# A one-core transformer layer: where two matrices' block sums are formed, and four small edits beside it

## The chip, the core and the metric

The kernel runs on one core of a Trainium2 chip. The metric is device time in microseconds (us) for one call, the median of several executions. Engines: PE multiplies matrices, DVE, ACT and POOL work on elements, SP issues nearly all DMAs.

## The reference

One layer (DEPTH = 1) on a 1024 x 1024 activation `x`, float32, 1024 frames in chunks of 64:

```python
h = rmsnorm(x, norm_mix_g)
qa, fa, ia, ga, qb, kb, vb, gate_a, gate_b = split(h @ w_in)          # w_in: 1024 x 5632
oa = hgrn2_mixer(qa, fa, ia, ga, ...)       # 4 heads of 128, decayed recurrence over chunks
ob = band_attention(qb, kb, vb, ...)        # 8 heads of 64, own chunk and 8 before it
merged = sigmoid(gate_a) * (oa @ w_branch_a) + sigmoid(gate_b) * (ob @ w_branch_b)
x = x + merged @ w_out
h2 = rmsnorm(x, norm_ffn_g)
x = x + (silu(h2 @ w_ffn_gate) * (h2 @ w_ffn_up)) @ w_ffn_down        # width 2816
h3 = rmsnorm(x, norm_ple_g)
x = x + sigmoid(h3 @ w_ple_gate) * (p @ w_ple_proj)
```

## The kernel before

Activations lie with features on the 128 partitions and 1024 frames along the free axis. Every float32 operand of a large product is split into a rounded part and a remainder (`wh`/`wl` for weights, whi/wlo for their halves and sums), and a product is three matmuls: hi x hi, hi x lo, lo x hi. ACT casts the rounded part, POOL or DVE subtracts to get the remainder.

The large products use a scheme with seven block products in place of eight (Strassen's, in a form with the sums S1 to S4 of weight blocks and T1 to T4 of activation blocks; `KINDS` lists the order A11, S2, A12, S3, S1, A22, S4).

The order of work on each engine is the program's order: `Pinned` and `order` chain each engine's instructions, and the generators (`yield`) say what is written between which products. The stages and about where they lie in the profile:

- `first_norm`, then `hgrn_in` and `hgrn_mix` for four heads, woven together: until about 310 us. `hgrn_in` projects, `hgrn_mix` runs the recurrence by levels (products of DVE, transposes through PE, copies of ACT). `hgrn_mix` copies the transposed keys with ACT at L447.
- `attention`: until about 527 us.
- `gate_units`: six units of seven products each for the mixer's gates, until about 690 us; then `branches`, `out_proj`, `first_part` and `second_part`.
- `ff_pairs`: 22 units n = 0 to 21, alternately gate and up, 84 matmuls each, about 893 to 1290 us (n = 0 is done in `second_part`). In a unit `strassen` writes seven `product`s into three PSUM banks b1 to b3; behind each, DVE adds a bank to a sum (`u2 = p1 + b2` behind product 1, two sums behind product 3, and so on), and `next(side)` lets one step of side work follow: `strassen_weights` prepares the next unit's weights, `keep_acts` stores the activations for the down product. Product 3 adds to the bank b2 that u2 was read from, so PE may start it only when DVE has made u2. DVE works in order, so what stands ahead of such a sum delays it.
- `ff_down` (seven passes with `passes`), then `ple`, seven passes again, with `side` doing norms and output work between the steps.

The sums S1 to S4 of the weights of `w_out` (four jobs, `oq`) and `w_ffn_down` (eleven jobs, `wq`) are formed ahead of their products: load four blocks, four additions, store the sums in DRAM (`spill`). `QUADS` = 8 jobs are done by `quad_early` beside the recurrence: `quad_piece` cuts a job in two halves, each one load, four additions of 128x256 on POOL (L1093), four stores; `beside` takes one step of it per step of `hgrn_in`. The other seven are done by `quad_slow` in `gate_units`, with four POOL additions of 128x512 a job (L1068 to L1079).

`unit_gate` makes a gate: DVE multiplies by the row of norms `rb`, ACT takes the Sigmoid, POOL multiplies twice. `Small` pools hold rings of temporaries: `FFN` (tmp, raw, q512, q1024), `MIXER`, `SMALL`. `weights(n, ahead)` loads the next weights into two raw buffers, which come free when POOL has made the remainder. In `ple`, `out` makes one block of the output in four steps (DVE product, ACT Sigmoid, DVE product, final add and DMA), `some(4)` takes one step of four such streams, and `m_split` casts and subtracts the next activation operand, which `operand` otherwise does when fewer than two are ready.

Of the kernel before, what the change touches and what calls it, by code (L numbers as in the profile page):

```python
# [17 lines left out]
P = 128  # L18
# [13 lines left out]
RAW = 2  # L32
AHEAD = 3
PLAIN = 4
QUADS = 8


C_MIX, C_FFN, C_PLE, C_ON, C_GQ, C_GK, C_LB = 0, 8, 16, 24, 25, 26, 27
# [18 lines left out]
class Trunk:  # L57
# [175 lines left out]
    def setup(self):  # L233
        nc, d = self.nc, self.d
        cp = self.cp
        self.cols = cp.tile([P, N_COL], F32, name="cols")
        nc.scalar.dma_start(self.cols, d["cols"])
        self.eye = cp.tile([P, P], F32, name="eye")
        self.ones = cp.tile([P, 1], F32, name="ones")
        nc.vector.memset(self.ones, 1.0)  # L240
        self.onesr = cp.tile([P, P], F32R, name="onesr")
        nc.vector.tensor_copy(self.onesr, self.ones[:, :].to_broadcast([P, P]))
        self.mhalf = cp.tile([P, 8], F32, name="mhalf")
        nc.vector.memset(self.mhalf, -0.5)
# [20 lines left out]
    def first_norm(self):  # L265

        nc = self.nc
        self.u = []
        outs = [self.mm() for _ in range(4)]
        start = [self.unit() for _ in range(2)]  # L270
        ws = [(hi, lo) for hi, lo, _, _ in start]
        for k in range(KC):
            x = self.slot()
            sc = self.cols[:, C_MIX + k:C_MIX + k + 1]
            if k == 0:

                hi, lo = self.slot(F32R), self.slot(F32R)
                h0, h1 = slice(0, HALF), slice(HALF, T)
                self.load(x[:, h0], self.d["x"][k][:, h0])
                for unit in start:  # L280
                    self.unit_piece(unit, 0, 2 * P)
                self.load(x[:, h1], self.d["x"][k][:, h1])
                for h in (h0, h1):
                    self.A.activation(hi[:, h], x[:, h], AF.Copy, scale=sc)
                    nc.vector.scalar_tensor_tensor(lo[:, h], x[:, h], sc, f32(hi[:, h]), ALU.mult, ALU.subtract)
                self.u.append((hi, lo))
            else:
                self.load(x, self.d["x"][k])
                self.u.append(self.split(x, sc, self.A))
            if k == 1:  # L290
                for unit in start:
                    self.unit_piece(unit, 2 * P, D)
            if k == 3:
                self.load(self.eye, self.d["eye"])
                self.load(self.masks, self.d["masks"])
# [12 lines left out]
        return outs  # L308
# [486 lines left out]
    def gate_units(self, sums):  # L795
# [42 lines left out]
        for n in range(units):  # L838

            def side():  # L840
                more = self.strassen_weights() if n + 1 < units else self.branch_first()
                if n == 0:
                    yield
                    yield
                next(more, None)
                if n + 2 < units:
                    self.strassen_load()
                yield
                for i, _ in enumerate(more):
                    for _ in range(1 + i % 2):  # L850
                        next(sums, None)
                    yield

            self.strassen(lambda c, half, ps: self.gate_done(PLAIN + 2 * n + c, half, ps), side(), early=n == 0)
# [225 lines left out]
            yield  # L1080
        store(*prev)

    def quad_piece(self, src, k, sums, half):

        G, cols = self.nc.gpsimd, HALF // 2
        w = self.slot(late=True)
        at = slice(half * cols, half * cols + cols)
        self.load(w[:, :].rearrange("p (i c) -> p i c", i=4), src.rearrange("p (i c) -> p i c", i=4)[:, :, at])
        for _ in range(5):
            yield  # L1090
        a11, a21, a22, a12 = [w[:, i * cols:i * cols + cols] for i in range(4)]
        for out, x, y, op in ((a22, a21, a22, ALU.add), (a21, a11, a21, ALU.subtract), (a11, a22, a11, ALU.subtract), (a12, a12, a11, ALU.subtract)):
            G.tensor_tensor(out, x, y, op)  # L1093
            yield
        yield
        to = slice(k % 2 * HALF + at.start, k % 2 * HALF + at.stop)
        for kind, part in zip(("S2", "S3", "S1", "S4"), (a11, a21, a22, a12)):
            if k % 2 == 0 and half == 0:
                sums[kind, k // 2] = self.spill()
            self.store(sums[kind, k // 2][:, to], part)  # L1100
        yield
        yield

    def quad_early(self, jobs):

        pieces = [self.quad_piece(*job, half) for job in jobs for half in range(2)]
        live = []
        while pieces or live:
            if pieces:
                live.append(pieces.pop(0))  # L1110
            for _ in range(6):
                for x in list(live):
                    if next(x, x) is x:
                        live.remove(x)
                yield

    def quad_plan(self, plain, npairs, sums):
# [286 lines left out]
    def unit_gate(self, c, half, ps):  # L1404
# [2 lines left out]
        hs = slice(half * HALF, half * HALF + HALF)  # L1407
        s = self.stmp()
        V.tensor_tensor(g[:, hs], ps, self.rb[:, hs], ALU.mult)
        A.activation(s, g[:, hs], AF.Sigmoid)  # L1410
        G.tensor_tensor(g[:, hs], g[:, hs], s, ALU.mult)
        G.tensor_tensor(g[:, hs], g[:, hs], self.rb[:, hs], ALU.mult)

    def unit_up(self, c, half, ps):
        hs = slice(half * HALF, half * HALF + HALF)
# [132 lines left out]
    def ff_pairs(self):  # L1548
        V, A, G = self.V, self.A, self.G

        units = len(self.sorder)
        self.acts = {}
        self.strassen_load()
        for n in range(1, units):
            if n % 2 == 0:
# [2 lines left out]
            def side():  # L1558
# [6 lines left out]
                yield  # L1565
                for _ in more:
                    next(keep, None)
                    yield
                drain(keep)

            self.strassen((self.unit_gate, self.unit_up)[n % 2], side())
            if n % 2 == 1:
# [28 lines left out]
    def down_first(self):  # L1601

        self.down_plan()
        self.ahead = 3
        self.weights(0, ahead=3)
        yield
        for _ in range(2):
            self.down_load()
            yield
        self.down_split()  # L1610
        self.down_load()
        yield
# [128 lines left out]
    def ple(self):  # L1741
# [32 lines left out]
        def after(kind, u, ps):  # L1774
# [10 lines left out]
            elif kind == "S1":  # L1785
                V.tensor_tensor(u3[u], ps, u3[u], ALU.add)
                V.tensor_tensor(ps, ps, u2[u], ALU.add)
                todo.append(out(2 * u + 1, h0, u3[u]))
            elif kind == "A22":
                todo.append(out(2 * u + 1, h1, ps))  # L1790
                next(todo[-1])
# [18 lines left out]
        def side():  # L1810
# [29 lines left out]
            yield  # L1840
            for i in range(4):
                some(4)
                yield
            del todo[:]

# [15 lines left out]
    def run(self):  # L1861
# [18 lines left out]
        with ExitStack() as es:  # L1880
# [10 lines left out]
            self.hg, self.ended, self.pend, self.qk, self.bias, self.ob = {}, [], [], {}, {}, []  # L1891
            self.oa = [None] * 4
            with ExitStack() as mixer:
                self.masks = mixer.enter_context(tc.tile_pool(name="levels", bufs=1)).tile([P, len(LEVELS), 64], U8, name="masks")
                outs = self.first_norm()
                self.xp = Small(tc, mixer, MIXER)
                self.late = mixer.enter_context(tc.tile_pool(name="late1", bufs=2))
                jobs = [(d["oq"][k], k, self.osums) for k in range(4)] + [(d["wq"][k], k, self.sums) for k in range(NFF // 2)]
                sums = self.quad_early(jobs[:QUADS])
                drain(beside(self.hgrn_in(0, outs), sums))  # L1900
                for h in range(3):
                    weave(beside(self.hgrn_in(h + 1), sums), self.hgrn_mix(h), 41500, 17000)
                self.feed = self.attn_in()
                weave(beside(chain(self.attn_v(), islice(self.feed, FIRST)), sums), self.hgrn_mix(3), 41500 + 1300 * FIRST, 17000)
                drain(sums)
                self.attn_setup()
                drain(self.attention())
            with ExitStack() as xs:
                self.qp = Small(tc, xs, QUARTERS, "gate_", reuse_waits="tile")
                self.fp = Small(tc, xs, FFN, "gates_", reuse_waits="tile")  # L1910
                drain(self.gate_units(self.quad_slow(jobs[QUADS:])))
            with ExitStack() as xs:
                self.late = xs.enter_context(tc.tile_pool(name="late", bufs=6, reuse_waits="tile"))
                drain(self.branches())
# [16 lines left out]
            drain(self.ple())  # L1931


SMALL = {"rb": 1, "rtok": 1, "epsv": 1, "state": 1, "t8": 2, "t4": 4, "mx2": 4, "den": 4}
QUARTERS = {"whiq": 3, "wloq": 3}
FFN = {"q1024": 1, "q512": 3, "raw": 2, "tmp": 8}
MIXER = {"s": 3, "pt": 4, "bias": 4, "qk": 4, "qs": 2, "sq": 1}


# [18 lines left out]
def beside(main, side):  # L1958
    for x in main:
        next(side, None)  # L1960
        yield x


def weave(main, side, main_ns, side_ns):
# [111 lines left out]
```

## Time and profile before

| | |
|---|---|
| median of three runs | 1590.09 us (1587.43, 1590.09, 1590.85) |
| profiled execution | 1588.19 us, span 1585.9 us |
| TensorE clock over the span | 0.996 |
| DMA | 230.40 MB, mean 145 GB/s |

In the rows, "A 12.0 (x3)" means busy for 12.0 us in 3 instructions; a group row gives count, busy us, mean ns of one, and the idle time before them with what ended it; in a timeline row stand start, duration, engine, line, operation and the tiles (out<-in). PEld is PE's weight load. Buffer numbers are left out of the names: `s` is a 128x1024 slot, `m` a small tile, `t` a temporary (stmp), `pm` a PSUM bank, `wr` raw weights, `q` sums of weights, `d` DRAM.

### The profile page before, as it was taken

How to read it: one execution, taken by the hardware profiler on the slowest of the kernel's cores; microseconds unless marked ns; L12 is line 12 of the kernel's file. 1: busy time of each engine (PE TensorE's matmuls, PEld its weight loads, DVE VectorE, ACT ScalarE, POOL GpSimd, SP SyncE). 2: the span in 40 equal slices, each digit the busy share in tenths (PEclk: the TensorE clock that was granted, in tenths of full speed). 3: DMA queues.
4: the chain of work that ended last, by engine and by line, in shares of the span. 5: the costliest groups of instructions: out<-in, count | busy, mean ns of one | idle time of the engine just before them, and what ended most of it. 6: DMA issues, size and time to landing. Idle time of an engine off the chain costs nothing.

```text
span 1585.9 us, 21744 instructions
## 1 busy us (share of the span) xinstructions
PE 1559.4 (98%) x8224; PEld 1311.1 (83%) x8224; DVE 1166.6 (74%) x1670; ACT 639.8 (40%) x1057; POOL 802.0 (51%) x461
## 2 busy tenths in 40 slices
PE   8999999999999999999999999999999999999997
PEld 6898888878888888888888888888888888888886
DVE  5656675468778778644898988888888856765658
ACT  6321211157777643421377322232222234445453
POOL 3764542123113059625330877777777754645454
PEclk9999999999999999999999999999999999999999
DMA  5443220220113358675244433333333278885344
GB/s 189 138 156 119 90 97 27 66 89 27 48 41 107 140 191 306 239 292 212 71 149 172 159 100 100 100 100 113 104 112 107 89 255 321 296 274 196 126 133 158
DMA packets 92649, 230.40 MB, mean 145 GB/s; under 512 B 9856, under 2 KB 26880, under 8 KB 92032
## 3 DMA queue, kind: packets, MB, share of 16 engines
q1 hardware_dynamic: 92400, 229.00, 42.1%
q8 instruction: 64, 1.05, 0.3%
q14 instruction: 41, 0.34, 0.1%
q10 hardware_dynamic: 144, 0.02, 0.0%
HBM read 163.70 MB, written 65.27 MB: 144 GB/s over the span
## 4 chain that ended last, share of the span: by engine, by line
PE 80%; DVE 6%; DMA 6%; POOL 4%; issue 2%; ACT 2%; SPq 1%; POOLq 0%; ACTq 0%; DVEq 0%
PE pm L83 77%; DVE s L54 3%; PE pm L86 3%; POOL wl L126 2%; DMA d<-s 1%; POOL s L1093 1%; DMA s<-in_oq 1%; DMA wr<-d 1%; DVE m L54 1%; SPq L78 1%; DMA wr<-in_qk 1%; DVE q L54 0%; POOL s L54 0%; ACT wh L123 0%; DMA wr<-in_fm 0%
## 5 line engine op out<-in xcount | busy, mean ns | idle before, releaser
L83 PE MATMUL pm<-s,wh 128*128 128x512 f32 (+1 forms) x1712 | 532.1, 392 | 6.6 <-ACT wh L123 5.2
L83 PE MATMUL pm<-s,whi 128*128 128x512 f32 x1568 | 483.0, 389 | 0.6 <-DVE t L54 0.6
L126 POOL TENSOR_TENSOR wl<-wr,wh 128x1024 fp32r<-128x1024 f32 (+2 forms) x108 | 269.5, 2500 | 321.1 <-ACT wh L123 314.9
L83 PEld LDWEIGHTS pm<-s,wh 128*128 128x128 f32 x1712 | 319.9, 189 | 73.5 <-ACT wh L123 5.6
L83 PEld LDWEIGHTS pm<-s,whi 128*128 128x128 f32 x1568 | 294.2, 188 | 61.9 <-DVE t L54 1.0
L83 PE MATMUL pm<-s,wl 128*128 128x512 f32 (+1 forms) x856 | 334.1, 390 | 0.3 <-POOL wl L126 0.3
L54 DVE TENSOR_TENSOR s<-s,s 128x512 f32<-128x512 f32 (+4 forms) x213 | 255.9, 1230 | 92.4 <-ACT s L54 58.3
L83 PE MATMUL pm<-s,wlo 128*128 128x512 f32 x784 | 305.2, 389 | 0.0
L83 PE MATMUL pm<-wh,s 128*128 128x256 f32 (+1 forms) x896 | 239.3, 341 | 0.0
L123 ACT CAST wh<-wr 128x1024 fp32r<-128x1024 f32 (+2 forms) x114 | 114.7, 1007 | 261.7 <-PE pm L83 132.8
L83 PEld LDWEIGHTS pm<-s,wl 128*128 128x128 f32 x856 | 161.3, 188 | 34.8 <-POOL wl L126 1.4
L83 PEld LDWEIGHTS pm<-s,wlo 128*128 128x128 f32 x784 | 147.2, 188 | 31.1 <-DVE wlo L54 0.5
L83 PEld LDWEIGHTS pm<-wh,s 128*128 128x128 f32 x896 | 155.4, 191 | 13.8
L83 PE MATMUL pm<-wl,s 128*128 128x256 f32 (+1 forms) x448 | 148.0, 330 | 0.4 <-POOL wl L126 0.4
L54 DVE TENSOR_TENSOR t<-pm,t 128x512 f32<-128x512 f32 x138 | 94.7, 686 | 71.4 <-PE pm L83 69.3
L54 POOL TENSOR_TENSOR wlo<-wr,whi 128x512 fp32r<-128x512 f32 (+1 forms) x53 | 109.9, 2083 | 72.2 <-ACT whi L54 72.2
L54 DVE TENSOR_TENSOR s<-pm,s 128x512 f32<-128x512 f32 (+1 forms) x134 | 87.3, 680 | 79.9 <-PE pm L83 78.7
L54 ACT CAST whi<-q 128x512 fp32r<-128x512 f32 (+1 forms) x81 | 61.5, 759 | 160.3 <-DVE q L54 140.5
L54 POOL TENSOR_TENSOR s<-s,t 128x512 f32<-128x512 f32 x44 | 76.6, 1741 | 81.7 <-ACT t L54 81.7
L54 ACT CAST s<-s 128x1024 fp32r<-128x1024 f32 (+1 forms) x94 | 90.2, 980 | 68.0 <-DVE s L54 33.7
L54 POOL TENSOR_TENSOR wlo<-q,whi 128x512 fp32r<-128x512 f32 x52 | 89.0, 1712 | 19.0 <-ACT whi L54 19.0
L83 PEld LDWEIGHTS pm<-wl,s 128*128 128x128 f32 x448 | 85.9, 192 | 5.9 <-POOL wl L126 0.6
(146 smaller groups left out, 1953.5 us busy)
## 6 DMA issues: line engine op xcount, KB each, us to landing
s<-d SPq DMA_DIRECT2D x67, 512.0 KB, 6.0
d<-s SPq DMA_DIRECT2D x115, 256.0 KB, 3.3
wr<-d SPq DMA_DIRECT2D x36, 512.0 KB, 3.7
s<-in_wq SPq DMA_DIRECT2D x22, 512.0 KB, 5.6
wr<-in_sg SPq DMA_DIRECT2D x22, 512.0 KB, 4.1
wr<-in_su SPq DMA_DIRECT2D x22, 512.0 KB, 4.1
s<-in_x SPq DMA_DIRECT2D x21, 512.0 KB, 7.8
d<-s SPq DMA_DIRECT2D x18, 512.0 KB, 4.9
```

The lines of the kernel that those rows point to most:

```text
L54: return lambda *a, **k: self.trunk.order(op(*a, **k), self.key)
L78: return self.order(self.nc.sync.dma_start(out, ap), "sp")
L83: return self.order(self.nc.tensor.matmul(*a, **k))
L86: return self.order(self.nc.tensor.transpose(*a, **k))
L123: self.nc.scalar.copy(hi[:, c], raw[:, c])
L126: rest.tensor_tensor(lo[:, c], raw[:, c], f32(hi[:, c]), ALU.subtract)
L1093: G.tensor_tensor(out, x, y, op)
```

## The change

Seven edits. (1) `quad_early`, `quad_piece` and `beside` go; five jobs are done by `quad_slow` in `gate_units` (one step per product, where it was one or two in turn), and the other ten by the new `quad_pieces` in `ff_pairs`, in halves, with the additions on DVE and one buffer `quad`; `tmp` has 7 buffers instead of 8. (2) `unit_gate` uses Silu, and POOL multiplies once. (3) `down_first` loads two weights ahead, then activations, then the third weight. (4) In `ple`, `m_split` is called in four steps of `side`. (5) The final add of the S1 outputs is on DVE. (6) `onesr` stands before `ones`, `masks` has 8 x 64 bytes instead of 5 x 64. (7) `state` stands before `rtok` in `SMALL`.

```diff
-QUADS = 8
+QUADS = 5
...
+        self.onesr = cp.tile([P, P], F32R, name="onesr")
         self.ones = cp.tile([P, 1], F32, name="ones")
         nc.vector.memset(self.ones, 1.0)
-        self.onesr = cp.tile([P, P], F32R, name="onesr")
...
@@ gate_units
-                for i, _ in enumerate(more):
-                    for _ in range(1 + i % 2):
-                        next(sums, None)
+                for _ in more:
+                    next(sums, None)
                     yield
@@ in place of quad_piece and quad_early
+    def quad_pieces(self, jobs):
+
+        V, cols = self.V, HALF // 2
+        for src, k, sums in jobs:
+            for half in range(2):
+                self.n += 1
+                w = self.fp.tile([P, 4 * cols], F32, tag="quad", name=f"qd{self.n}")
+                at = slice(half * cols, half * cols + cols)
+                self.load(w[:, :].rearrange("p (i c) -> p i c", i=4), src.rearrange("p (i c) -> p i c", i=4)[:, :, at])
+                yield
+                yield
+                a11, a21, a22, a12 = [w[:, i * cols:i * cols + cols] for i in range(4)]
+                V.tensor_tensor(a22, a21, a22, ALU.add)
+                V.tensor_tensor(a21, a11, a21, ALU.subtract)
+                yield
+                V.tensor_tensor(a11, a22, a11, ALU.subtract)
+                V.tensor_tensor(a12, a12, a11, ALU.subtract)
+                yield
+                for kind, part in zip(("S2", "S3", "S1", "S4"), (a11, a21, a22, a12)):
+                    if k % 2 == 0 and half == 0:
+                        sums[kind, k // 2] = self.spill()
+                    self.store(sums[kind, k // 2][:, k % 2 * HALF + at.start:k % 2 * HALF + at.stop], part)
                 yield
@@ unit_gate
-        A.activation(s, g[:, hs], AF.Sigmoid)
-        G.tensor_tensor(g[:, hs], g[:, hs], s, ALU.mult)
-        G.tensor_tensor(g[:, hs], g[:, hs], self.rb[:, hs], ALU.mult)
+        A.activation(s, g[:, hs], AF.Silu)
+        G.tensor_tensor(g[:, hs], s, self.rb[:, hs], ALU.mult)
@@ ff_pairs
+        pieces = self.quad_pieces(self.later)
...
                 for _ in more:
                     next(keep, None)
+                    if n > 1:
+                        next(pieces, None)
                     yield
                 drain(keep)
+                if n % 4 == 0:
+                    next(pieces, None)
+                if n == units - 2:
+                    drain(pieces)
@@ down_first
-        self.weights(0, ahead=3)
+        self.weights(0, ahead=2)
         yield
         for _ in range(2):
             self.down_load()
             yield
+        self.weights(0, ahead=3)
@@ ple
-                todo.append(out(2 * u + 1, h0, u3[u]))
+                todo.append(out(2 * u + 1, h0, u3[u], V))
...
             yield
             for i in range(4):
                 some(4)
+                self.m_split()
                 yield
             del todo[:]
@@ run
-                jobs = [(d["oq"][k], k, self.osums) for k in range(4)] + [(d["wq"][k], k, self.sums) for k in range(NFF // 2)]
-                sums = self.quad_early(jobs[:QUADS])
-                drain(beside(self.hgrn_in(0, outs), sums))
+                drain(self.hgrn_in(0, outs))
...
-                drain(self.gate_units(self.quad_slow(jobs[QUADS:])))
+                jobs = [(d["oq"][k], k, self.osums) for k in range(4)] + [(d["wq"][k], k, self.sums) for k in range(NFF // 2)]
+                drain(self.gate_units(self.quad_slow(jobs[:QUADS])))
+                self.later = jobs[QUADS:]
...
-SMALL = {"rb": 1, "rtok": 1, "epsv": 1, "state": 1, "t8": 2, "t4": 4, "mx2": 4, "den": 4}
+SMALL = {"rb": 1, "state": 1, "rtok": 1, "epsv": 1, "t8": 2, "t4": 4, "mx2": 4, "den": 4}
-FFN = {"q1024": 1, "q512": 3, "raw": 2, "tmp": 8}
+FFN = {"q1024": 1, "q512": 3, "raw": 2, "tmp": 7, "quad": 1}
```

More of the change, by code (lines that the diff above doesn't have):

```diff
@@ L294, in first_norm @@
                 self.load(self.eye, self.d["eye"])
-                self.load(self.masks, self.d["masks"])
+                self.load(self.masks[:, :len(LEVELS), :], self.d["masks"])
             if k:
@@ L1081, in quad_slow @@
         store(*prev)
[L1083 to L1114, printed above, removed]
+    def quad_pieces(self, jobs):
[19 more added lines that the diff above has]
+                    self.store(sums[kind, k // 2][:, k % 2 * HALF + at.start:k % 2 * HALF + at.stop], part)
@@ L1893, in run @@
             with ExitStack() as mixer:
-                self.masks = mixer.enter_context(tc.tile_pool(name="levels", bufs=1)).tile([P, len(LEVELS), 64], U8, name="masks")
+                self.masks = mixer.enter_context(tc.tile_pool(name="levels", bufs=1)).tile([P, 8, 64], U8, name="masks")
                 outs = self.first_norm()
@@ L1897, in run @@
                 self.late = mixer.enter_context(tc.tile_pool(name="late1", bufs=2))
-                jobs = [(d["oq"][k], k, self.osums) for k in range(4)] + [(d["wq"][k], k, self.sums) for k in range(NFF // 2)]
-                sums = self.quad_early(jobs[:QUADS])
-                drain(beside(self.hgrn_in(0, outs), sums))
+                drain(self.hgrn_in(0, outs))
                 for h in range(3):
-                    weave(beside(self.hgrn_in(h + 1), sums), self.hgrn_mix(h), 41500, 17000)
+                    weave(self.hgrn_in(h + 1), self.hgrn_mix(h), 41500, 17000)
                 self.feed = self.attn_in()
-                weave(beside(chain(self.attn_v(), islice(self.feed, FIRST)), sums), self.hgrn_mix(3), 41500 + 1300 * FIRST, 17000)
-                drain(sums)
+                weave(chain(self.attn_v(), islice(self.feed, FIRST)), self.hgrn_mix(3), 41500 + 1300 * FIRST, 17000)
                 self.attn_setup()
@@ L1955, in drain @@
             return e.value
[L1958 to L1961, printed above, removed]
 def weave(main, side, main_ns, side_ns):
```

## The prediction

> **What bounds the kernel now.** I read the page first, then busy times by stage, PE's waits, and then single stretches of the timeline in which PE waits or nearly does.
>
> ```profile
> span 1585.9 us, 21744 instructions
> PE 1559.4 (98%) x8224; PEld 1311.1 (83%) x8224; DVE 1166.6 (74%) x1670; ACT 639.8 (40%) x1057; POOL 802.0 (51%) x461
> ```
>
> PE is busy in all but 26.5 us of the span, and the change neither adds nor removes a matmul. So the change can only move those 26.5 us, plus time in which PE runs at a lower clock, or make PE wait where it doesn't wait now. Where they lie shows by stage (busy us of each engine, then clock, DMA share, GB/s):
>
> ```profile
> 43.00:240.00 197.00, 191.33 (x1405) 174.89 (x1404) 132.70 (x228) 43.93 (x79) 109.09 (x93) 0.99 0.37 121
> 527.00:690.00 163.00, 163.00 (x738) 134.64 (x735) 119.18 (x136) 68.11 (x99) 89.56 (x53) 1.00 0.72 251
> 866.00:893.00 27.00, 26.17 (x117) 21.53 (x117) 26.37 (x25) 16.13 (x25) 18.81 (x10) 0.94 0.59 195
> 893.00:1274.00 381.00, 381.00 (x1682) 315.57 (x1681) 334.18 (x308) 109.43 (x161) 286.05 (x163) 1.00 0.31 101
> 1556.00:1586.00 30.00, 19.63 (x98) 16.54 (x97) 24.98 (x34) 8.19 (x14) 15.74 (x10) 0.90 0.28 107
> 173.00:180.00 7.00, 6.74 (x44) 6.74 (x45) 1.77 (x7) 1.33 (x4) 1.44 (x2) 0.76 0.01 2
> ```
>
> The recurrence of the first three heads (43 to 240) holds 5.7 us of idle PE; the gate units of the mixer (527 to 690) hold none; the gate/up units of the feed-forward part (893 to 1274) hold none, though DVE is busy 88% there; the last 30 us hold 10.4. The last row is the one place in the recurrence with a lower clock: 7 us at 0.76 lose 7 x 0.24 = 1.7 us. So a change that empties the recurrence's side work can win at most 5.7 + 1.7 = 7.4 us there, and whatever it moves into 893 to 1274 can win nothing there and only lose.
>
> **The recurrence: 64 additions of POOL and their 80 DMAs go.** QUADS 8 with quad_early means 8 x 2 pieces of four additions.
>
> ```profile
> L1093 POOL TENSOR_TENSOR s<-s 128x256 f32<-128x256 f32 x64 | 55.8, 873 | 52.4 <-DMA s<-in_wq 24.4 <-DMA s<-in_oq 21.4 <-DMA d<-s 2.9
> PE pm L83 <- ACT s L447: 3.2, 2, 1.8
> PE pm L83 <- DVE s L54: 1.3, 3, 0.5
> PE pm L86 <- DVE s L54: 0.8, 1, 0.8
> 156.04 1.98 POOL L1093 TENSOR_TENSOR s<-s 128x256 f32<-128x256 f32 x2
> 157.98 2.82 POOL L126 TENSOR_TENSOR wl<-wr,wh 128x1024 fp32r<-128x1024 f32 x1
> 161.01 4.25 POOL L1093 TENSOR_TENSOR s<-s 128x256 f32<-128x256 f32 x4 [0.21 <-DMA s<-in_wq]
> 162.65 2.01 DVE L54 TENSOR_TENSOR m<-s,s 128x512 f32<-128x512 f32 x2
> 164.58 2.92 DVE L54 TENSOR_TENSOR s<-s,s 128x512 f32<-128x512 f32 x2
> L54 DVE TENSOR_TENSOR s<-s 128x512 f32<-128x512 f32 x10 | 6.8, 684 | 0.0
> 173.26 0.81 PE L83 MATMUL pm<-s,s 128*128 128x128 f32 x4 [1.76 <-ACT s L447]
> ```
>
> The second to fourth rows are PE's waits of this stage: for ACT's copy of the transposed keys, and for DVE's products. Both follow on DVE: ACT casts what DVE made. A 128x512 product of two SBUF tiles costs DVE 0.68 alone (the row of ten), and the pairs at 162.65 and 164.58 took 2.01 and 2.92 where 1.37 would do, the first and half of the second beside POOL's additions at 161.01. Of these 2.2 us of delay I put 1.2 down to L1093, and 0.7 more to its additions at 156.04 and around 169: 1.9 us of DVE lag ahead of PE's waits of 0.8 and 1.76 us. Without it PE's two waits there shrink by about 1.9, and with a shorter wait I expect the slow clock behind it (1.7) to go in most cases: 1.2. The same in the other heads: of the remaining 3.1 us of idle (5.7 - 2.6) I take half, 1.7. Sum **-4.8 us**; the ends are -1.3 (only half of 2.6: the split of weights at 157.98, 2.82 us, and the small splits stay on POOL and block DVE as before) and -7.4 (all). SP is passed by 16 loads and 64 stores fewer ahead of the weights; PE waits for no DMA here, so nothing is counted.
>
> **The mixer's gate units** get 5 whole jobs instead of 7, so eight additions fewer (row L1068 is one of four a job), at one step per product instead of one or two. FFN's tmp ring is 7, not 8: at the next unit's first copy it reuses u2 instead of p1, which DVE reads last some 3 us after the unit's end, while the copy comes 2.7 us after it. PE is idle for 0.0 of 163 us here, so there is no gain; 0 taken, ends 0 and +1.5 (six units at a quarter of a microsecond).
>
> ```profile
> L1068 POOL TENSOR_TENSOR s<-s,s 128x512 f32<-128x512 f32 x7 | 10.1, 1445 | 3.4 <-DMA d<-t 2.0 <-DMA d<-s 1.4
> L54 POOL TENSOR_TENSOR s<-s,rb 128x512 f32<-128x512 f32 x41 | 68.2, 1663 | 3.2
> L54 ACT ACTIVATE t<-s 128x512 f32<-128x512 f32 x44 | 27.8, 632 | 116.4 <-DVE s L54 112.4 <-issue 2.6 <-ACT whi L54 0.2
> L54 ACT ACT_TABLE_LOAD x2 | 2.6, 1283 | 0.0
> 1582.00 0.42 DVE L54 TENSOR_TENSOR s<-s,s 128x256 f32<-128x256 f32 x1
> d<-s SPq DMA_DIRECT2D x64, 128.0 KB, 3.8
> s<-in_wq SPq DMA_DIRECT2D x22, 512.0 KB, 5.6
> 990.94 1.42 DVE L54 TENSOR_TENSOR t<-pm,t 128x512 f32<-128x512 f32 x2 [1.44 <-PE pm L83]
> 996.38 0.69 DVE L54 TENSOR_TENSOR t<-pm,t 128x512 f32<-128x512 f32 x1 [0.17 <-PE pm L83]
> 997.83 2.88 DVE L54 TENSOR_TENSOR q<-wr,q 128x512 f32<-128x512 f32 x1
> 1005.74 0.68 DVE L54 TENSOR_TENSOR t<-pm,t 128x512 f32<-128x512 f32 x1
> ```
>
> **The gate/up units** lose one POOL multiplication per gate, 44 in all (41 of them in the row, 1.66 each: 68 us), because Silu does the work of Sigmoid and one product. No Silu is in the trace; the same shape takes 0.63 with Sigmoid, and I take that. It may need its table in and Sigmoid's back, 2 x 1.28 us on ACT, which is busy 29% of 893 to 1274 and idle before these activations: 0 taken, with no gain since no wait of PE here ends on ACT, and at most +1.3 ahead of 893, where DVE is full.
>
> They gain 10 jobs x 2 pieces = 20 pieces: 80 DVE additions of 128x256 at 0.42 (the row of the last stage) = 34 us, 20 loads and 80 stores on SP. DVE has 381 - 334 = 47 us free there, and POOL's relief gives some of its blocked time back, so there is room on the average. What counts is one deadline. The adds at 990.94 and 996.38 start when PE ends products 3 and 5 of a unit: 2.72 us a product. Product 1 of the next unit ends five products after 990.94, at 1004.5; its sum u2 ran at 1005.74 to 1006.42, and product 3, which adds to the same bank, is due at 1007.2. Slack 0.8 us. From 996.38 to 1006.42 DVE does eight operations, 5.4 us alone, in 10.0: 4.6 us are blocking, as at 997.83, where 0.68 became 2.88. A piece's pair (0.84) in this window would use the slack up, if POOL blocked as now; with one POOL operation in two gone from the gate's end it should block about a fifth less, 0.9. That cancels out: 0 for the additions.
>
> [...]
>
> The wait added: one buffer (quad: 1), so a load stands on SP behind the landing of its predecessor's four stores, and strassen_load and keep_acts' stores stand behind it for 3.8 us; those have a unit (19 us) of lead. The stores' issue (1.4), landing (3.8) and the load (5.6, less in this emptier stage) make 8 to 10.8 us from a piece's last addition to the next one's first; DVE comes to it three steps later, 8.2 us, or 13.6 where a unit's end lies between. With five steps a unit and four a piece I count 7 of 20 pieces with no unit's end between. DVE's queue would stand there for 0 to 2.6 us, the PSUM sums behind it, and PE behind those beyond the slack. I take 0.2 each: **+1.4 us**; ends 0 and 7 x 1.8 = +12.6.
>
> **Ahead of 893** and at the start of the down stage:
>
> ```profile
> 892.67 0.50 PE L83 MATMUL pm<-s,whi 128*128 128x512 f32 x1 [0.58 <-DVE t L54]
> 1320.81 0.50 PE L83 MATMUL pm<-s,wl 128*128 128x512 f32 x1 [0.34 <-POOL wl L126]
> 1263.69 13.01 SPq L78 DMA_DIRECT2D wr<-in_dw  x3
> ```
>
> The wait at 892.67 is the same u2 add, late behind POOL's gate products; with one of two gone I take it as gone, **-0.6** (ends -0.7, +0.7 with the table load). In down_first SP stood 13 us in three weight loads, the third waiting for a raw buffer, with the activations' loads behind it; with two loads first those start some 12 us sooner and crowd less at 1320: **-0.2** of 0.34 (ends -0.4, +0.4).
>
> **The last stage.** m_split is called once more in each of the four steps behind `some(4)`. Counting side()'s steps, these lie in the fourth product (S3), not the fifth. Three casts and remainders (T4 twice, B22's first) move from the two passes behind it to there. The final adds of the S1 outputs move from POOL to DVE.
>
> ```profile
> 1556.51 1.21 DVE L54 TENSOR_TENSOR s<-s,s 128x1024 fp32r<-128x1024 f32 x1
> 1557.65 4.70 DVE L54 TENSOR_TENSOR s<-s,rb 128x512 f32<-128x512 f32 x4
> 1563.98 5.82 DVE L54 TENSOR_TENSOR s<-s,s 128x1024 fp32r<-128x1024 f32 x5 [1.64 <-ACT s L54]
> 1565.89 6.32 POOL L54 TENSOR_TENSOR s<-s,s 128x512 f32<-128x512 f32 x4 [5.90 <-DVE s L54]
> 1569.73 2.48 DVE L54 TENSOR_TENSOR pm<-pm,rb 128x512 f32<-128x512 f32 x4
> ```
>
> From 1563.98 DVE is never idle for long until the end, so its lag is the tail. The remainder at 1556.51 (1.21) leaves; the one at 1563.98 stays (B22's second). ACT comes to its cast some 0.8 sooner. Then four products of 0.6 and four new adds of 0.6 take 4.8 where the row has 4.7 for the products alone, blocked by POOL's adds of 1.6: **-0.5 us**, ends -1.2 and +1.5 (the adds unhidden, POOL's blocking still there).
>
> **Alignment** moves onesr, state, masks and what lies behind them by some bytes.
>
> ```profile
> L83 PEld LDWEIGHTS pm<-m,onesr 128*128 128x128 f32 x24 | 4.5, 188 | 1.0
> L83 PEld LDWEIGHTS pm<-s,wh 128*128 128x128 f32 x1712 | 319.9, 189 | 73.5 <-ACT wh L123 5.6 <-DVE s L196 1.7 <-DVE s L285 0.8
> ```
>
> onesr now lies behind a tile of 4 bytes and loads in 188 ns, as long as the large tiles: 0.
>
> **The sum**: -4.8 - 0.6 - 0.2 - 0.5 + 1.4 = -4.7. The profiled execution took 1588.2 (span 1585.9 and 2.3 around it), which gives 1583.5; it stands 1.9 under the median of the three runs, 1590.1 (1587.4 to 1590.9), and against that median I say **1585.4 us**.
>
> **Rivals.** *The deadline of u2 (slower).* The additions of the pieces stand in DVE's queue ahead of the PSUM sums in all 16 units that carry pieces (5 steps a unit, 81 steps, from the third on). If POOL blocks as before, a unit is late by 0.84 - 0.8 plus one block of the short additions, some 0.7: 16 x 0.7 = 11.2, and 1590.1 - 6.1 + 11.2 = 1595.2. It decides from 0.4 us a unit on (6.4 us, the whole gain). For it: DVE's 88% and 0.8 us of slack; against it: 68 us fewer on POOL. Chance 0.27. [...]
> *The recurrence stays.* POOL's weight splits, now sooner, block DVE in the additions' place; only 1.3 is won there: 1590.1 - 1.3 - 1.3 + 1.4 = 1588.9. Chance 0.18.
> *All of it comes*: 7.4 in the recurrence, 0.6, 0.4 and 1.2 after it, no loss in the units: 1580.5. Chance 0.08.
>
> **How the numbers follow.** The forecast has 0.47, its own range 1582 to 1588.5. What a measurement of this kernel tells from no change is about 0.2%, 3.2 us: faster is under 1586.9. Faster: 0.38 of the forecast, 0.08, and 0.03 of the second rival, 0.49; within: 0.09 + 0.12 + 0.03 of the first, 0.24; slower: 0.24 + 0.03, 0.27. The range takes in the third rival and most of the first: 1580 to 1597.
>
> **What would show it.** Right: no L1093 row, idle of PE in 43 to 240 under 3 us and a clock of 1.00 there; POOL with one product per gate; DVE over 90% in the units and PE still without a wait; the last DVE add half a microsecond nearer to PE's end. Wrong: PE waits for DVE t in the units, DVE waiting there for a load of wq, or the waits for ACT's L447 as long as before.

## The result, and the profile after

The changed kernel takes 1609.49 us (median of 6 runs, 1607.23 to 1615.12) where the kernel before takes 1589.93 (6 runs): 1.0127 times as long, 95% interval 1.0099 to 1.0155. The forecast was 1585.4 and the range ended at 1597. The profiled execution took 1614.1 us, 4.6 more than the median.

The page after, its head and the first line of engines:

```profile
span 1611.1 us, 21725 instructions
...
PE 1568.1 (97%) x8224; PEld 1314.9 (82%) x8224; DVE 1165.9 (72%) x1754; ACT 639.6 (40%) x1059; POOL 649.6 (40%) x341
```

POOL is 152 us less busy, DVE as busy as before, and PE idles 43.0 us instead of 26.5. Busy times by stretch (recurrence, feed-forward units, and 16 us out of these), columns as in the prediction:

```profile
43.00:240.00 197.00, 195.11 (x1454) 179.66 (x1454) 123.46 (x229) 44.10 (x80) 54.33 (x29) 1.00 0.12 38
...
893.00:1296.00 403.00, 385.86 (x1662) 314.86 (x1661) 340.48 (x384) 104.31 (x156) 211.16 (x119) 0.98 0.44 147
1046.00:1062.00 16.00, 12.99 (x45) 10.16 (x44) 12.23 (x13) 1.98 (x3) 7.65 (x4) 0.79 0.28 98
```

The recurrence is now nearly full (1.9 us of idle PE instead of 5.7, clock 1.00). The gate/up units, in which PE had no idle time, have 17 us of it and a lower clock, although DVE is busy only 84% of the time and POOL only 52%. PE's waits in the units, after:

```profile
PE pm L83 <- DVE t L54: 17.1, 12, 3.0
```

Both traces hold all 8,224 matmuls, so the start of each can be compared with the start of the same one before. The differences below are worked out that way, by where the matmul stood before; "on POOL" is the version of the experiments with the additions on POOL.

| from .. to (us, before) | after | on POOL |
|---|---|---|
| start .. 45 | +2.1 | -0.6 |
| 45 .. 526 (recurrence, attention) | -7.3 | -7.5 |
| 526 .. 859 (mixer's gate units to the out projection) | +0.1 | +0.1 |
| 859 .. 909 (first gate/up units) | +0.6 | +0.7 |
| 909 .. 1287 (the other gate/up units) | +26.9 | +0.7 |
| 1287 .. 1488 (down stage) | -0.7 | -0.7 |
| 1488 .. last matmul | +3.0 | +1.1 |
| behind the last matmul (10.30 us before) | +0.4 | +0.6 |
| sum; difference of the spans | +25.1; +25.2 | -5.6; -5.5 |

One line decides, the fifth. All 12 of its waits lie in the ten up units n = 3 to 21, seven ahead of product 3 and five ahead of product 5, and none in a gate unit. The longest of them, on PE, then DVE's queue and POOL's queue in front of it:

```profile
1055.04 1.22 PE L83 MATMUL pm<-s,whi 128*128 128x512 f32 x2 [3.01 <-DVE t L54]
1056.06 0.63 PE L83 MATMUL pm<-s,wlo 128*128 128x512 f32 x1
```

```profile
1045.63 0.68 DVE L54 TENSOR_TENSOR q<-wr 128x512 f32<-128x512 f32 x1
1046.23 2.95 DVE L54 TENSOR_TENSOR qd<-qd 128x256 f32<-128x256 f32 x2
1049.10 3.42 DVE L54 TENSOR_TENSOR wlo<-q,whi 128x1024 fp32r<-128x1024 f32 x1
1052.45 1.94 DVE L54 TENSOR_TENSOR qd<-qd 128x256 f32<-128x256 f32 x2
1054.30 1.41 DVE L54 TENSOR_TENSOR t<-pm,t 128x512 f32<-128x512 f32 x2
```

```profile
1045.72 1.75 POOL L54 TENSOR_TENSOR wlo<-q,whi 128x512 fp32r<-128x512 f32 x1
1047.42 4.01 POOL L54 TENSOR_TENSOR wlo<-wr,whi 128x512 fp32r<-128x512 f32 x2
```

This is how such a wait is read. PE stands at product 5 of an up unit, which adds to the bank that u3 (t<-pm,t at 1054.30) must have read. u3 is short and its operand, product 3, has long been done; what is late is its place in DVE's queue. Ahead of it stand a piece's two pairs of additions (qd<-qd), 4.9 us where 4 x 0.42 would do, and a remainder (wlo) of 3.42 us that takes 1.2 alone. Beside them POOL computes remainders without a pause. Behind the wait a matmul takes 0.63 instead of 0.39: the clock, 0.79 over these 16 us.

### The profile page after: what moved, and what is told of

The parts are those of the page before. It is cut to its first block, busy times and chain, and to the rows that moved or that the text cites. A ratio compares the mean times of both kernels' runs of the same rounds, so it can differ in the third digit from the quotient of the medians.

```text
span 1611.1 us, 21725 instructions
## 1 busy us (share of the span) xinstructions
PE 1568.1 (97%) x8224; PEld 1314.9 (82%) x8224; DVE 1165.9 (72%) x1754; ACT 639.6 (40%) x1059; POOL 649.6 (40%) x341
## 5 line engine op out<-in xcount | busy, mean ns | idle before, releaser
L83 PE MATMUL pm<-s,whi 128*128 128x512 f32 x1568 | 489.1, 394 | 19.9 <-DVE t L54 19.9
L126 POOL TENSOR_TENSOR wl<-wr,wh 128x1024 fp32r<-128x1024 f32 (+2 forms) x108 | 264.9, 2458 | 407.0 <-ACT wh L123 396.9
L83 PEld LDWEIGHTS pm<-s,whi 128*128 128x128 f32 x1568 | 296.0, 190 | 86.7 <-DVE t L54 25.4
L54 DVE TENSOR_TENSOR s<-s,s 128x512 f32<-128x512 f32 (+4 forms) x217 | 263.2, 1243 | 96.2 <-ACT s L54 58.7
L83 PEld LDWEIGHTS pm<-wh,s 128*128 128x128 f32 x896 | 156.4, 193 | 13.7
L54 POOL TENSOR_TENSOR wlo<-wr,whi 128x512 fp32r<-128x512 f32 (+1 forms) x53 | 116.1, 2199 | 95.4 <-ACT whi L54 95.4
L54 POOL TENSOR_TENSOR s<-t,rb 128x512 f32<-128x512 f32 x44 | 70.4, 1602 | 115.2 <-ACT t L54 115.2
L54 POOL TENSOR_TENSOR wlo<-q,whi 128x512 fp32r<-128x512 f32 x52 | 82.7, 1590 | 78.9 <-ACT whi L54 72.8
L54 ACT ACTIVATE t<-s 128x512 f32<-128x512 f32 x44 | 27.8, 633 | 167.3 <-DVE s L54 164.4
```

The costliest lines, as they stand in the source:

```text
L54: return lambda *a, **k: self.trunk.order(op(*a, **k), self.key)
L83: return self.order(self.nc.tensor.matmul(*a, **k))
L126: rest.tensor_tensor(lo[:, c], raw[:, c], f32(hi[:, c]), ALU.subtract)
```

## Experiments

Theory A: the additions of the pieces stand in DVE's queue ahead of PSUM sums that PE waits for, at the one place where DVE has no room. Rivals: the pieces' transfers with their single buffer (B); ACT, where the copy of p1 stands behind the gate's last activation (C); the mere amount of work for DVE.

**Additions left out.**

```
-                V.tensor_tensor(a22, a21, a22, ALU.add)
-                V.tensor_tensor(a21, a11, a21, ALU.subtract)
                 yield
-                V.tensor_tensor(a11, a22, a11, ALU.subtract)
-                V.tensor_tensor(a12, a12, a11, ALU.subtract)
                 yield
```

> The changed kernel with the four additions of each piece left out: the 20 loads and 80 stores of the pieces stay in the feed-forward part, only the 80 DVE additions go, so that the sums of the later weights hold the raw weights. Theory A (the additions stand in DVE's queue ahead of the PSUM sums that PE waits for at products 3 and 5 of the up units): nearly all of the 27 us that the feed-forward part lost comes back, waits of PE for DVE there under 2 us, time 1582 to 1587. Theory B (the loads and stores of the pieces, with one buffer, hold up the queue of SP or DVE): nothing comes back, 1605 to 1612. Theory C (ACT: the gate's last activation holds up the copy of p1, by Silu or its place): only the waits at product 3 matter and they stay, some 8 us, so about 1592 to 1600.

1583.37 us (ratio 0.9951, 0.9935 to 0.9967). By stretch:

```profile
893.00:1270.00 377.00, 377.00 (x1665) 312.18 (x1664) 294.12 (x304) 107.69 (x159) 221.34 (x120) 1.00 0.48 160
```

PE has no idle time and full clock, with all 100 transfers of the pieces in place (DMA share 0.48, as large as ever). B falls, and C too, since Silu and ACT's order are unchanged. The additions alone cost the 27 us.

**The same additions on POOL.**

```
-                V.tensor_tensor(a22, a21, a22, ALU.add)
+                self.nc.gpsimd.tensor_tensor(a22, a21, a22, ALU.add)
... (the other three likewise)
```

> The changed kernel with the pieces' 80 additions on POOL instead of DVE, at the same steps. Theory A: the PSUM sums have no piece ahead of them any more, but POOL's additions (0.87 us each in the recurrence, 70 us in all) still exclude DVE's operations on SBUF, so that a part of the loss stays: 1584 to 1594, PE's waits for DVE in the up units under 8 us. Theory B: 1605 to 1612 as before. If the exclusion alone made the loss, whichever engine adds: 1605 or more too, and then PE's waits for DVE t stay at 15 us or more.

1583.52 us (0.9963, 0.9942 to 0.9983): this version beats both kernels, the one before by some 6 us. The groups of the additions and the stretch:

```profile
L1094 POOL TENSOR_TENSOR qd<-qd 128x256 f32<-128x256 f32 x20 | 20.1, 1004 | 49.2 <-DMA qd<-in_wq 49.2
L1098 POOL TENSOR_TENSOR qd<-qd 128x256 f32<-128x256 f32 x20 | 20.0, 999 | 1.4
L1097 POOL TENSOR_TENSOR qd<-qd 128x256 f32<-128x256 f32 x20 | 18.3, 917 | 1.6
L1095 POOL TENSOR_TENSOR qd<-qd 128x256 f32<-128x256 f32 x20 | 17.2, 861 | 1.5
```

```profile
893.00:1267.00 374.00, 373.93 (x1648) 309.04 (x1647) 313.88 (x303) 108.62 (x159) 289.76 (x198) 1.00 0.48 161
```

75.6 us of additions, no shorter than on DVE (73.0), and PE loses 0.1 of 374 us. POOL even stands 49 us waiting for pieces to land, and nobody waits for it. DVE's own work takes 20 us longer than without any additions (313.88 against 294.12 in a stretch 3 us shorter), so POOL's additions still hold DVE up; that does not matter as long as no PSUM sum stands behind it.

**The move of the sums alone**, with Sigmoid and two products of POOL as before:

```
-        A.activation(s, g[:, hs], AF.Silu)
-        G.tensor_tensor(g[:, hs], s, self.rb[:, hs], ALU.mult)
+        A.activation(s, g[:, hs], AF.Sigmoid)
+        G.tensor_tensor(g[:, hs], g[:, hs], s, ALU.mult)
+        G.tensor_tensor(g[:, hs], g[:, hs], self.rb[:, hs], ALU.mult)
... (and the down stage's start and the last stage as before)
```

> The move of the sums alone (with the smaller ring and the aligned tiles): the gate function is Sigmoid and two products of POOL again, and the down stage's start and the last stage are as before. Theory A: the loss in the feed-forward part is there, and larger by the blocking of 44 more POOL products (68 us of POOL): 27 to 40 us lost there, 1610 to 1622. Theory C (Silu causes the waits): no loss there, 1583 to 1590. If the relief of POOL by Silu did nothing: 1607 to 1611, as with all edits.

1634.46 us (1.0273, 1.0257 to 1.0288), more than was expected; 55 us are lost in the units. PE's waits there and the additions:

```profile
PE pm L83 <- DVE t L54: 37.1, 14, 4.9
```

```profile
L54 DVE TENSOR_TENSOR qd<-qd 128x256 f32<-128x256 f32 x78 | 81.0, 1038 | 1.3
```

In the changed kernel the same group stands at 912 ns, and at 420 where POOL rests. So POOL's work lengthens what stands ahead of the sums. Silu is no cause; without its relief the move costs twice as much.

**All edits but the move:**

> The kernel before with every edit but the move of the sums: Silu, the order of loads at the down stage's start, the two edits of the last stage, the aligned tiles. The sums stay in the recurrence on POOL. Theory A: no wait of PE in the units; the time is that of before with the small terms, by the comparison of the two traces +0.6 at 866 to 893, -0.7 at the down stage's start, +0.5 at the tail, and +3.0 at the last stage if that wait belongs to its edits: 1590 to 1594. If that 3 us wait is one of phase: 1587 to 1591. Theory C: 1597 or more.

1593.92 us (1.0014, 0.9997 to 1.0030; 1588.3 to 1597.2): no difference that this shows, and no wait of PE in the units. In its profile nothing is won between 45 and 526 (+2.3), and in that of the move alone all of it (-7.5), so the recurrence's gain belongs to the move.

**Place against amount.** One piece a unit, at its first two steps, and the additions carried out in one kind of unit only:

```
-                V.tensor_tensor(a22, a21, a22, ALU.add)
-                V.tensor_tensor(a21, a11, a21, ALU.subtract)
+                if self.at_unit % 2 == 0:      # gate units; == 1 in the other kernel: up units
+                    V.tensor_tensor(a22, a21, a22, ALU.add)
+                    V.tensor_tensor(a21, a11, a21, ALU.subtract)
... (the second pair likewise)
-                    if n > 1:
+                    if n > 1 or i > 2:
+                        self.at_unit = n
                         next(pieces, None)
...
-                if n % 4 == 0:
-                    next(pieces, None)
```

> The changed kernel with every piece's two pairs of additions at the first two steps of a unit (one piece a unit, same loads and stores), and carried out only where the unit is a gate unit, 11 pieces of 20; the other 9 pieces keep their loads and stores and lose their additions, so the sums of the later weights are partly raw. In the changed kernel's trace DVE's additions at this place of the gate units took 0.42 us each, and POOL is idle there. Theory A (it is where the additions stand in DVE's queue that costs): the feed-forward part loses under 3 us, 1582 to 1587. If it is the mere number of additions (half of them, half the loss): 1595 to 1598.

> The same steps, the additions carried out only in the up units, 9 pieces of 20. There DVE has no idle time in the first four products, POOL is busy, and pairs at this place of the changed kernel took 1.5 and 1.4 to 2.5 us; the two up units that had them there waited 3.2 and 2.7 us and lost 1 to 2.5 more at half clock. Theory A: 9 x 3 to 5 us lost, 1610 to 1630. If it is the mere number of additions: 1593 to 1597.

Gate units: 1587.93 us (0.9985, 0.9974 to 0.9995), slightly over what was expected (its profile loses 2.2 between 859 and 909, ahead of the pieces, and 1.8 at the down stage's start, behind the late one); up units: 1609.76 (1.0125, 1.0111 to 1.0139), at the lower end. Between 927 and 1248 the gate version loses 0.00 us; the other loses 25.4, which is 2.8 for each of the nine up units. Its waits, the group of its additions and DVE's queue in one unit:

```profile
PE pm L83 <- DVE t L54: 22.7, 9, 2.5
```

```profile
L54 DVE TENSOR_TENSOR qd<-qd 128x256 f32<-128x256 f32 x36 | 43.7, 1214 | 0.6
```

```profile
1007.29 4.05 DVE L54 TENSOR_TENSOR qd<-qd 128x256 f32<-128x256 f32 x2
1011.26 2.31 DVE L54 TENSOR_TENSOR wlo<-q,whi 128x1024 fp32r<-128x1024 f32 x1
1013.49 0.87 DVE L54 TENSOR_TENSOR qd<-qd 128x256 f32<-128x256 f32 x2
1014.28 1.41 DVE L54 TENSOR_TENSOR t<-pm,t 128x512 f32<-128x512 f32 x2
```

The gate version's additions at the same steps, and its group (which holds one late piece in an up unit too):

```profile
1022.05 0.88 DVE L54 TENSOR_TENSOR qd<-qd 128x256 f32<-128x256 f32 x2
1023.68 1.42 DVE L54 TENSOR_TENSOR t<-pm,t 128x512 f32<-128x512 f32 x2 [0.75 <-PE pm L83]
```

```profile
L54 DVE TENSOR_TENSOR qd<-qd 128x256 f32<-128x256 f32 x44 | 21.6, 492 | 0.8
```

The same two pairs take 4.05 + 0.87 us in an up unit and 0.88 + 0.88 in a gate unit, where DVE has 0.75 us to spare right behind a pair. In an up unit of the kernel before, u3 starts after 0.29 us of idle DVE and must end before product 5:

```profile
1010.05 1.42 DVE L54 TENSOR_TENSOR t<-pm,t 128x512 f32<-128x512 f32 x2 [0.29 <-PE pm L83]
```

Product 3 has ended there at about 1010.0, product 4 takes 2.72, and the first add 0.7: 2.0 of slack and 0.3 of idle. 4.9 of additions less 2.3 is 2.6; the waits are 2.5. Amount falls as an explanation, place stands.

**Is Silu's relief what makes POOL's room?** The additions on POOL, with Sigmoid and two products (the edit shown above):

> The version with the additions on POOL, but the gate function as before: Sigmoid and two products of POOL. It asks whether Silu's relief is what makes POOL's room. POOL would be busy 286 us as before plus 80 x 0.87 = 70 of 381, 93%. Theory A with the room made by Silu: POOL becomes late with the remainders of the weights and blocks DVE more, 1590 to 1615. If POOL's room was there anyway: 1582 to 1586, as with Silu.

1612.78 us (1.0144, 1.0131 to 1.0158). The stretch and PE's waits from 890 on:

```profile
890.00:1290.00 400.00, 386.42 (x1666) 314.61 (x1665) 344.13 (x304) 108.66 (x159) 354.29 (x239) 0.99 0.46 152
```

```profile
PE pm L83 <- POOL wlo L54: 9.2, 6, 1.6
PE pm L83 <- DVE t L54: 4.1, 6, 1.9
```

POOL is busy 354 of 400 us and PE waits for its remainders. So the move needs both: Silu's relief, and the additions on the engine that Silu relieves.

**The small terms.** The version on POOL with the last stage as before:

> The version with the additions on POOL, and the two edits of the last stage undone (no earlier remainders, the last additions on POOL). In the runs with these edits PE loses 1.0 to 3.0 us around 1513 of the kernel before, and none in the one run without them. If they are the cause: 1.0 to 1.5 us better than with them, 1581 to 1583. If not: 1583 to 1584.5.

1583.62 us (0.9963, 0.9951 to 0.9976), not to be told from 1583.52; the loss near 1513 stays (1.3), so the last stage's edits are not its cause. With the old order of loads at the down stage's start:

> The version with the additions on POOL, with the loads at the start of the down stage in the order of before (three weights, then the activations). All runs with the new order lose 0.9 to 3.0 us of PE near 1513 of the kernel before, with the last stage's edits and without them; the one run with the old order loses none. If the order of loads is the cause: that loss goes, and the loss at the start of the down stage comes back by 0 to 0.7: 1582 to 1583.5. If not: the loss near 1513 stays, 1583 to 1584.5.

1586.0 us (0.9972, 0.9960 to 0.9983). The loss near 1513 is gone in this profile (0.0), as expected of a cause, but the time isn't better. With Silu's table loaded early:

```
+                self.A.activation(self.warm, self.ones, AF.Silu)
                 drain(self.out_proj())
```

> The version with the additions on POOL, with one more activation: Silu of a 128x1 tile ahead of the out projection, so that Silu's table is loaded there, where ACT has idle time, and not in front of the first gate (1.28 us on ACT in the changed kernel). If the table load is what makes PE's wait at the second unit's third product 1.3 to 2.8 us instead of 0.6: that wait falls to 0.6 or less and 0.7 to 2.5 us are won, 1581 to 1583. If the order of DVE's and POOL's work makes it: the wait stays over 1.2 us and the time at 1583 to 1584.5.

1583.41 us (0.9963, 0.9950 to 0.9976). That is no better than 1583.52, though in the profile nothing is lost now between 847 and 927 (0.0 instead of +0.8); PE's wait for DVE from 860 on:

```profile
PE pm L83 <- DVE t L54: 0.6, 1, 0.6
```

With this and both old orders together:

> Candidate for the best: the additions on POOL, Silu with its table loaded early, the down stage's start and the last stage as before. By the single terms (-7.5 in the recurrence, -0.6 at the start of the feed-forward part, +0.7 in its units, 0 behind it): 1582 to 1583. If the small terms are phases that change with every edit: 1582 to 1585.

1584.47 us (0.9966, 0.9952 to 0.9979), no better than its parts; in its profile PE waits 2.1 us around 885, early table or not, and 1.3 are lost near 1513, old order or not. At last, with the same two old orders and the early table, each piece on the engine that has room at its place:

```
+                E = V if self.at_unit % 2 == 0 else self.nc.gpsimd
+                E.tensor_tensor(a22, a21, a22, ALU.add)
... (the other three likewise, at the first two steps of each unit)
```

> As the candidate for the best, with one piece a unit at its first two steps: on DVE in the gate units, where the same additions cost 0.00 us a unit, and on POOL in the up units. Theory A (only the place in a queue counts, not the engine): no wait of PE in the units, 1581 to 1583, as the candidate or 0.7 better. If POOL's additions in the up units, at steps where POOL has no idle time, hold up its remainders or exclude DVE's operations there: waits of 0.5 to 2 us in each up unit, 1587 to 1600.

1590.24 us (1.0009, 0.9998 to 1.0020): a miss, but not by the mechanism that was named. Between 927 and 1248 the units lose 0.00 us, better than on POOL alone (0.7). 8 us are lost at the start of the down stage, some 2 of them to half clock, which holds from 1283.95 for 6.8 us:

```profile
PE pm L83 <- ACT s L54: 2.9, 1, 2.9
PE pm L83 <- DVE s L54: 1.6, 1, 1.6
PE pm L83 <- DVE t L54: 0.6, 1, 0.6
```

With these steps the twentieth piece ends in the last up unit; its additions still count to the gate unit ahead, so they are on DVE and take 4.8 us there. On SP its stores wait for its additions until 1269.6; the down stage's weights stand behind them (1271.5), and behind a third weight load, in the old order, the activations, from 1279.2 on. PE waits for the cast of the first. The gate version, with the same late piece and the new order, loses 1.8 there. One piece fewer in these units was not tried.

## Why the prediction was wrong, point by point

**The gate/up units: the step that failed.** "Slack 0.8 us ... That cancels out: 0 for the additions." Three things in it:
- The piece's pair was charged at 0.84, the additions' length alone. In the first five products of the changed kernel's up units 21 of 30 additions took 1.4 to 2.5 each; the mean of all 80 is 912 ns. "Blocked about a fifth less" was an average over POOL's work, and what went of POOL's work went from the gate's end, while the remainders that block an up unit stayed.
- Only u2's deadline was weighed. u3's, at product 5, has more slack (2.0), but two pairs stand ahead of it; 10.0 of the 17.1 us were waited there.
- "Room on the average" (47 us of free DVE) said nothing about the place. One pair of units of the kernel before, cut into the gate unit, products 0 to 3 of the up unit, and its products 4 to 6, would have shown it:

```profile
980.00:999.05 19.05, 19.05 (x86) 15.78 (x85) 17.19 (x19) 6.14 (x9) 9.80 (x6) 1.00 0.36 131
999.05:1009.93 10.88, 10.88 (x50) 9.01 (x49) 10.64 (x8) 4.20 (x7) 10.72 (x7) 1.00 0.32 89
1009.93:1018.10 8.17, 8.17 (x38) 6.77 (x37) 5.92 (x7) 0.58 (x1) 8.09 (x6) 1.00 0.19 59
```

DVE (third figure of busy time) has 1.9 and 2.3 us to spare in the first and the last cut and 0.2 in the middle, where POOL is busy 10.72 of 10.88 too. The gate version and the up version are this difference, 0.00 against 2.8 us a unit.

What of DVE's work POOL lengthens stands in the traces. In that of the kernel before, a sum with a PSUM input (t<-pm,t) takes 0.69 us beside POOL (62 of them in the units) and 0.68 with POOL at rest (46); one of two SBUF tiles (q<-wr,wr) takes 1.78 beside POOL (19 in the units) and 0.68 at 876.83, where POOL rests. A piece's addition takes 0.42 in a gate unit with POOL at rest, 1.51 and 2.51 in an up unit beside its remainders, and in the changed kernel each addition of 0.9 us or more ends 0.28 us behind the end of an instruction of POOL. From n = 2 on DVE was busy 330.2 us before, and 33.6 for the additions alone would make 363.8; it was 342.3. So 21.5 us of blocking did go, and such a sum says nothing of the deadlines.

**The rival of the deadline** was the case that came, with a chance of 0.27 and a price of 11.2 us (the 6.1 in its sum is the forecast's without the wait: 4.8 + 0.6 + 0.2 + 0.5). The price failed in its factors: 0.7 us a unit over 16 units. It was 26.9: 17.1 of waits, all in the ten up units, and the rest slower matmuls behind them, among them some 6 us in the three stretches of half clock at 1054, 1099 and 1136 (13.7 us long). This rival had no term for the clock behind a wait: the five waits of 0.85 us and less were followed by no half clock, but most were longer, and those of 2.1 to 3.0 were followed by it (the row of 0.79 is one). The number of units was miscounted as well: a piece takes five steps, not four, so that there is about one in each of 20 units.

**The wait added (+1.4)** did not come: in the changed kernel DVE stood 1.4 us ahead of the 80 additions in all, and the version without additions shows that the transfers cost PE nothing.

**The recurrence (-4.8)** went the right way and was sized too small: -7.3 in the table, -7.5 in the profiles of the runs without additions, on POOL, and of the move alone. Of it 6.3 lies in the prediction's stretch, up to 240, near its upper end of 7.4: two thirds of the idle time went, and the clock drop with its 1.4 to 1.7; 1.0 more came behind 240, which no term held. (Half of 3.1 is 1.55 and not 1.7, a slip that changes nothing.) The waits up to 240, after:

```profile
PE pm L83 <- DVE s L54: 1.5, 3, 0.5
PE pm L83 <- ACT s L447: 0.4, 2, 0.2
```

**Ahead of 893 (-0.6)** it became +0.6: the wait grew from 0.58 to 2.8, while the half clock at 866 to 870, worth 1.6, went. The table load was taken at 0 with +1.3 as its end; two more loads are there (four in this row, two before):

```profile
L54 ACT ACT_TABLE_LOAD x4 | 5.1, 1283 | 2.5 <-DMA d<-t 2.4
```

With the load early this wait was 0.6 in one version and 2.1 in another, where the nearest versions without that edit have 1.3 and 2.9; so the load seems to be 0.7 of it. But with the load in place and the sums in the recurrence there was none, and with Sigmoid, without the load, and the additions on POOL it was 1.3. What else sets it stays open.

**The mixer's gate units (0)** held: +0.1 from 526 to 859. **The down stage's start (-0.2)** came as -0.7, but -0.6 stands in profiles with the old order too, so it isn't the order's. **The last stage (-0.5)** came as +0.4 behind the last matmul; that tail is 10.1 to 11.1 us in runs with its edits and 10.3 to 10.8 without, which tells nothing apart. The +3.0 near 1513 was in no term. It is 0.0 to 3.6 from kernel to kernel, with each of the two edits and without; what sets the wait there stays open. Part of both this and the +2.1 at the start, where the version on POOL, with the same code there, has -0.6, is the clock: the changed kernel's profile has half clock from 1525.35 for 3.41 us and from 37.13 for 6.83 us, which lose 1.7 and 3.4; the up version's profile has such a stretch at that place too, from 1522.56 on, that of the kernel before has none.

## What to carry to other kernels

Price an instruction that is put into a queue by its length beside what runs there, not alone, and by what stands behind it: list for each place in the period which result is due next and how much slack it has. An engine's free share over a stage is no room; the same additions cost nothing in one half of a unit pair and 2.8 us a unit in the other. Work moved off one engine's critical stretch belongs on an engine for which no near deadline waits, even where it takes no less time there (75.6 us on POOL, 73.0 on DVE).

## What the runs showed of the hardware that was not expected

The half clock does not follow the length of a wait alone. In the up version nine waits of 2.5 us left the clock at full speed; in the changed kernel waits of 2.1, 2.5 and 3.0 us were each followed by half clock (1.7, 1.7 and some 3 us lost by it), and waits of 2.8 and 1.7 by none.

The traces show what differs. From 15 us on, up to the last matmul, every stretch of half clock in the traces of the kernel before and of the changed kernel is 3.41 us long or twice that, and within one trace these stretches start whole multiples of 3.413 us apart (in the changed kernel at 37.13, 1054.31, 1098.68, 1136.23 and 1525.35, in the kernel before at 173.74 and 866.64). So in these traces the clock changes on a grid of this step, which does not lie alike in every run: the up version's is 0.6 us off the changed kernel's. From 890 us on, in these two traces, the steps at full clock that held 1.95, 2.10, 2.28 and 2.43 us of idle PE were followed by half clock, and those that held 1.67 or less were not. Ahead of 890 idle time alone does not tell: steps with 0.26 and 0.69 us of it were followed by half clock too (from 866.64 before, 37.13 after). The up version has the comparison for one length of wait. Its nine waits stand 40.9 us apart, about 12 steps, and each lies across an edge of the grid, with at most 1.84 us of it in one step. A tenth wait of the same length, at another place of the program, lies with 2.49 us in one step, and half clock follows from 1522.56 on:

```profile
1522.59 2.08 PE L83 MATMUL pm<-eye,m 128*128 128x128 f32 x8 [2.52 <-POOL m L1729]
1522.56:1525.97 3.41, 3.38 (x12) 3.09 (x13) 0.00 (x0) 1.86 (x3) 2.06 (x1) 0.50 0.77 272
```

So in these three traces a wait counted, from 890 us on, by how much of it fell into one step of 3.413 us: up to 1.67 without half clock behind it and from 1.95 on with it, while in between 1.84 stood without it, and ahead of 890 a step with 1.76 was followed by it (at 173.74 in the kernel before). No kernel was made to move a wait against the grid; the bounds are read off the waits that occurred.
